# Start addresses of matmul operands: pools at multiples of 128 bytes, and some split weights 64 bytes further

## The chip, the cores and the metric

The kernel runs on one core of one Trainium2 chip. The metric is device time in microseconds (us) of one execution, the median of several runs. A profile is one execution taken with the hardware profiler; all times of single instructions come from it.

TensorE (PE in the profile) multiplies: a matmul holds one operand fixed in the array (the *stationary* operand, 128 columns here, loaded by its own instruction, PEld in the profile) and streams the other through it (the *moving* operand, 256 or 512 columns in nearly all of this kernel). Both are read from SBUF, the on-chip memory of 128 partitions; the sum goes to PSUM. The other engines are VectorE (DVE), ScalarE (ACT), GpSimd (POOL) and SyncE (SP, which only issues DMAs here).

## The reference

A two-layer backbone over 512 latent tokens of width 1024 with 256 context tokens: layer 0 has neighbourhood attention and a bidirectional gated recurrence (HGRN2), layer 1 a gated short convolution, and each layer ends in a convolutional gated feed-forward block. Nearly all the work is in the projections around them:

```python
for layer in range(DEPTH):                       # DEPTH = 2
    h = modulate(rms_norm(x, norm_mix_w[layer]), shift_m, scale_m)
    if is_even:
        y, y_ctx = even_mixer(h, h_ctx, w_in, w_out, rpb, lb, hg_norm_w, ctx_feeds_later)
    else:
        y = short_conv_mixer(h, od_w_in, od_conv_w, od_conv_b, od_w_out)
    x = x + gate_m[:, None, :] * y
    h = modulate(rms_norm(x, norm_ffn_w[layer]), shift_f, scale_f)
    x = x + gate_f[:, None, :] * conv_ffn(h, w_up, conv_w, conv_b, w_down)   # gelu(dwconv3(a)) * val
return rms_norm(x, final_norm_w)
```

All is float32. `conv_ffn` has an up projection to 2 x 2816 columns and a down projection from 2816 rows.

## The kernel before

**Split products.** A float32 operand `a` is split into `hi` (rounded to the matmul's reduced float32 type, `F32R`) and `lo = a - hi`. A product is three matmuls, `hi*hi + hi*lo + lo*hi`. The helper `mm3` (lines 287 to 290) issues them: L288 is weights-hi with moving-hi, L289 weights-hi with moving-lo, L290 weights-lo with moving-hi. So the moving tile alternates between the two halves of one activation, and the weights are loaded anew for each.

**Weights.** `Weights` (lines 41 to 142) walks a list `plan`: each entry is a list of DMA sources and a list of pieces. `_load` (L58) brings an entry into one of two `wraw` tiles by DMA from SP's queue. `conv` (L69) makes the next piece: ACT casts it into a `whi` tile (L92), DVE subtracts into `wlo` (L93); three `whi` and three `wlo` tiles of 128 x 1024 float32 take turns in the pool `wp`. `_block` (L99) does the same for the feed-forward's up projection, which computes a group of columns by Strassen-like combinations (names S1 to S4, A11, A12, A22, W1, W2; L125 and L126 write the split). `HOME` says which blocks share a tile: S1 to A22 lie in two halves of 512 columns of a tile, W1 and W2 each fill one. S1, S2, S3, S4, A11, A12 and A22 meet moving operands of 256 columns (half the tokens), W1 and W2 of 512. Three more pairs of weight tiles, listed in `ws.spare` (L1050), lie in the pool `gq` and are used at the end of each `project_back`.

**Which matmul uses what as weights.** In most stages the split weights are stationary and the activations move: `proj`, `pair`, `project_back` (512 columns; its last piece in two halves of 256), `quad` (two halves of 256) and `group` (the Strassen products). In two places it is turned round, activations stationary and weights moving with 256 columns: the value projection of layer 0 (`pvl`, `pvc`, L577 to L579) and the last down projection (`pd`, L1339 to L1341).

**Order.** Instructions are issued in the order in which the code is written, PE's order included; `Weave` interleaves the attention and recurrence tasks with the projections. Weights are converted a few pieces ahead of the matmuls that use them.

**Addresses.** Tiles of a pool lie one behind the other, each width rounded up to 32 bytes, and pools lie one behind the other too. So a small tile in an early pool moves everything behind it. In the program as built, with offsets in bytes modulo 128: the activations `h`, `hf`, `hm` (pool `yp`), the context `hc` (`mp`), the mixer outputs and most feed-forward outputs `g` (`zp`, `gp`) and the attention operands `KS`, `QS` start at 0; `wraw`, `whi` and `wlo` in `wp` at 64, because the pool `cp` ends at 64; the pools stacked from the other end (`xp`, `fp`, `gq`) at 96, so the Strassen combinations `T2` to `T4`, the spare weight tiles and the first six feed-forward outputs `g` are at 96; the weights `w0h`, `w0l` of the first projection (a temporary pool) at 96 as well.

Of the kernel before, what the change touches and what calls it, by code (L numbers as in the profile page):

```python
# [9 lines left out]
F32 = mybir.dt.float32  # L10
F32R = mybir.dt.float32r
# [3 lines left out]
ALU = mybir.AluOpType  # L15
AX = mybir.AxisListType
PSUM = bass.MemoryType.PSUM

P = 128
D = 1024  # L20
# [3 lines left out]
FF = 2816  # L24
# [17 lines left out]
class Weights:  # L42


    def __init__(self, nc, pool, plan):
        self.nc, self.pool, self.plan = nc, pool, plan
        self.subs = [(c, s) for c, (_, subs) in enumerate(plan) for s in range(len(subs))]
        self.half = {}
        self.raw = {}
        self.ready = []  # L50
        self.nsub = 0
        self.nload = 0
        self.ncall = 0
        self.spare = []
        self.pin = lambda i: i

    def _load(self):
# [8 lines left out]
        self.raw[self.nload] = views  # L66
        self.nload += 1

    def conv(self):  # L69

        if self.nsub >= len(self.subs):
            return
        c, s = self.subs[self.nsub]
        nm = self.plan[c][1][s]
        while self.nload <= min(c + 1 + (nm == "W2"), len(self.plan) - 1):
            self._load()
        if isinstance(nm, str):
            self._block(c, nm)
            return
        i, k0, k1, c0, c1 = self.plan[c][1][s]  # L80
        n, w = k1 - k0, c1 - c0
        if self.spare:
            pool, th, tl = self.spare.pop(0)
            hi = pool.tile([P, 1024], F32R, tag=th, name=f"whi{self.nsub}")
            lo = pool.tile([P, 1024], F32R, tag=tl, name=f"wlo{self.nsub}")
        else:
            hi = self.pool.tile([P, 1024], F32R, tag="whi", name=f"whi{self.nsub}", bufs=3)
            lo = self.pool.tile([P, 1024], F32R, tag="wlo", name=f"wlo{self.nsub}", bufs=3)
        hv = hi[:, : n * w].rearrange("p (k c) -> p k c", c=w)
        lv = lo[:, : n * w].rearrange("p (k c) -> p k c", c=w)  # L90
        rv = self.raw[c][i][:, k0:k1, c0:c1]
        self.nc.scalar.copy(hv, rv)  # L92
        self.pin(self.nc.vector.tensor_tensor(lv, rv, hv.bitcast(F32), ALU.subtract))  # L93
        self.ready.append((hv, lv))
        self.nsub += 1
# [4 lines left out]
    def _block(self, c, nm):  # L100


        V = self.nc.vector
        quarters = self.raw[c][0]
        A21, A22, A11, A12 = (quarters[:, 0, 512 * i : 512 * i + 512] for i in range(4))
        if nm == "S1":
            s3 = self.pool.tile([P, 512], F32, tag="ws3", name=f"ws3{self.nsub}", bufs=1)
            V.tensor_tensor(s3[:], A11, A21, ALU.subtract)
            self.half["S3"] = s3[:]
            V.tensor_tensor(A21, A21, A22, ALU.add)  # L110
        elif nm == "S2":
            V.tensor_tensor(A21, A21, A11, ALU.subtract)
        elif nm == "S4":
            V.tensor_tensor(A21, A12, A21, ALU.subtract)
        if nm in ("W1", "W2"):
            at = 1024 * (nm == "W2")
            src = self.raw[c + 1][0][:, 0, at : at + 1024]
        else:
            src = {"A11": A11, "A12": A12, "A22": A22, "S3": self.half.get("S3")}.get(nm, A21)
        key, z = self.HOME[nm]  # L120
        if z in (None, 0):
            self.half[key] = [self.pool.tile([P, 1024], F32R, tag=t, name=f"{t}{self.nsub}", bufs=3) for t in ("whi", "wlo")]
        at = 512 * (z or 0)
        hi, lo = (t[:, at : at + src.shape[-1]] for t in self.half[key])
        self.nc.scalar.copy(hi, src)  # L125
        V.tensor_tensor(lo, src, hi.bitcast(F32), ALU.subtract)  # L126
        self.ready.append(tuple(t.rearrange("p (g k c) -> p g k c", g=2, c=P) for t in (hi, lo)))
        self.nsub += 1
# [46 lines left out]
def backbone(ctx: ExitStack, tc: tile.TileContext, a, out, dump=None):  # L175
    nc = tc.nc
    V, S, G, TE = nc.vector, nc.scalar, nc.gpsimd, nc.tensor
# [5 lines left out]
    x, ctxt = a["xT"], a["ctxT"]  # L183
    ada_w = a["ada_w"]
    w_in, w_out = a["ev_w_in"][0], a["ev_w_out"][0]
    od_in, od_out = a["od_w_in"][0], a["od_w_out"][0]
    up, down = a["ffn_w_up"], a["ffn_w_down"]


    cp = ctx.enter_context(tc.tile_pool(name="cp", bufs=1))  # L190
    wp = ctx.enter_context(tc.tile_pool(name="wp", bufs=2))
    ap_ = ctx.enter_context(tc.tile_pool(name="ap_", bufs=1))
# [6 lines left out]
    def cols(w, c0):  # L199
        return [([ktiled(w)[:, :, c0 : c0 + 256]], [(0, 0, w.shape[0] // P, j, j + P) for j in (0, P)])]  # L200
# [7 lines left out]
    def wide(w, k0, k1, c0):  # L208
        n = k1 - k0
        return ([ktiled(w)[:, k0:k1, c0 : c0 + 256]], [(0, i, min(i + 4, n), 0, 256) for i in range(0, n, 4)])  # L210

    kgroups = [(0, 6), (6, 14), (14, 22)]
    plan = []
# [8 lines left out]
        plan += cols(w_out, 256 * j)  # L222

    def ffn_up_plan(l):
        r = cols(up[l], 0) + cols(up[l], FF)
        for j in range(FT // 2 - 1):
            q = [a["upq"][l, j, i][:, None, :] for i in range(2)]
            r += [([q[0]], QORDER), ([q[1]], [])]
        return r
# [2 lines left out]
    for j in range(4):  # L232
        plan += [rows_cols(down[0], k0, k1, 256 * j) for k0, k1 in kgroups]
    for j in range(4):
        plan += cols(od_in, D + 256 * j) + cols(od_in, 2 * D + 256 * j) + cols(od_in, 256 * j)
    for j in range(4):
        plan += cols(od_out, 256 * j)
    plan += ffn_up_plan(1)
    for j in range(4):
        plan += [wide(down[1], k0, k1, 256 * j) for k0, k1 in ((0, 8), (8, 16), (16, 22))]  # L240
    ws = Weights(nc, wp, plan)


# [1 line left out]
    ident, sel = cst[:, 0:128], cst[:, 128:256]  # L245
# [11 lines left out]
    oml = cp.tile([P, 8], F32, name="oml")  # L257
    noml = cp.tile([P, 8], F32, name="noml")
    amul = cp.tile([P, 5, KT], F32, name="amul")
    rowv = lambda i, n: pv[:, i : i + n]  # L260


# [211 lines left out]
    class Ada:  # L474
# [3 lines left out]
        n, calls, raw, late = 0, 0, {}, []  # L478
# [9 lines left out]
        def unit(self, aux):  # L488
            self.calls += 1
            while self.late and self.late[0][0] <= self.calls:  # L490
                self.late.pop(0)[1]()
            if self.n >= 8 * len(self.jobs):
                return
            r = self.n % 8
            l, p_, j = self.jobs[self.n // 8]
            while len(self.raw) < min(self.n + 3, 8 * len(self.jobs)):
                self.load()
            raw = self.raw[self.n]
            self.n += 1
            if r == 0:  # L500
                self.acc = ap_.tile([P, T], F32, tag="aacc", name=f"aa{self.n}", bufs=1)
                pin(V.tensor_scalar(self.acc[:], raw[:], sil[:, 0, 0:1], None, ALU.mult))
                return
            pin(V.scalar_tensor_tensor(self.acc[:], raw[:], sil[:, r, 0:1], self.acc[:], ALU.mult, ALU.add))  # L504
            if r < 7:
                return
            red = ap_.tile([P, 16], F32, tag="ared", name=f"ad{self.n}", bufs=1)
            V.tensor_reduce(red[:], self.acc[:].rearrange("p (b j) -> p b j", j=32), axis=AX.X, op=ALU.add,
                            apply_transpose=True)
            pm = []  # L510

            def gather():
                pm.append(aux(f"pad{l}{p_}{j}"))
                TE.matmul(pm[0][:, 0:16], sel, red[:], start=True, stop=True)

            def finish():
                c = p_ * 8 + 4 * j
                for qd in range(4):
                    s4 = slice(32 * qd, 32 * qd + 32)
                    V.tensor_tensor(mod[s4, l, c : c + 4], pm[0][s4, qd:16:4], abT[s4, l * 48 + c : l * 48 + c + 4],  # L520
                                    ALU.add)
                if p_ in (1, 4):
                    w0 = (16 if p_ == 1 else 32) + 8 * l + 4 * j
                    V.scalar_tensor_tensor(amul[:, 2 * l + (1 if p_ == 1 else 2), 4 * j : 4 * j + 4], mod[:, l, c : c + 4],
                                           1.0, pv[:, w0 : w0 + 4], ALU.add, ALU.mult)

            self.late += [(self.calls + 3, gather), (self.calls + 5, finish)]

    ada = Ada()
# [225 lines left out]
    for h in range(4):  # L755
        for d in range(2):
# [3 lines left out]
            s = hp.tile([P, T], F32, tag="s", name=f"s{h}{d}", bufs=2)  # L760
# [209 lines left out]
                wv.tick()  # L970


    xp = ctx.enter_context(tc.tile_pool(name="xp", bufs=1, side="right", reuse_waits="tile"))
    xT = [xp.tile([P, T], F32, name=f"xT{k}") for k in range(KT)]
    for k in range(KT):
        nc.sync.dma_start(xT[k][:], x[k * P : (k + 1) * P, :])
    fp = ctx.enter_context(tc.tile_pool(name="fp", bufs=1, side="right", reuse_waits="tile"))
# [300 lines left out]
    for j in range(4):  # L1278
# [6 lines left out]
        for i in range(2):  # L1285
            t = gp.tile([P, T], F32, tag=f"g{16 + i}", name=f"cs{j}{i}")
# [6 lines left out]
        for i in range(2):  # L1293
            m = 2 * j + i
            V.tensor_tensor(cs[i][:], ou[i][:], cs[i][:], ALU.mult)
            t = fp.tile([P, T], F32, tag="t", name=f"sc{m}", bufs=5)
# [30 lines left out]
    for i in range(4):  # L1327
        for k2 in range(2):
# [1 line left out]
            for k in range(4):  # L1330
                TE.transpose(pt[:, k * P : (k + 1) * P], xT[4 * k2 + k][:, i * P : (i + 1) * P], ident)
            S.copy(xk[i][:, k2 * T : (k2 + 1) * T], pt[:])
    ss = fp.tile([P, 4, 8], F32, tag="ss", name="ssf")

    def down(o, w, i, k0):
        ts = slice(i * P, (i + 1) * P)
# [13 lines left out]
    subs = range(0, FT, 4)  # L1350
# [77 lines left out]
```

## Time and profile before

| | |
|---|---|
| time of three runs | 1332.36 us median (1330.21 to 1336.62) |
| the profiled execution's own time | 1333.99 us |
| its span, first to last instruction | 1332.2 us |
| PE: busy, idle | 1304.5 us, 27.7 us |
| PE weight loads busy | 1147.6 us |
| DVE, ACT, POOL busy | 965.4, 625.2, 84.3 us |
| granted TensorE clock, mean | 0.995 |
| DMA | 172.35 MB, mean 129 GB/s |

The duration that the profile gives for one matmul (0.39 us for 512 columns, 0.28 us for 256) includes its way through the array; matmuls overlap. What the stream costs is the distance from one start to the next, called a *step* below. It is read from the view of stretches, where a row names a stretch of the span, its length, PE's busy time and, behind x, the number of matmuls that touch the stretch. Those that only reach in at an edge are counted too, so the number is one to three above the number of steps.

### The profile page before, as it was taken

Reading aid. Unit: us, or ns where it says so; the run is one execution under the profiler, and the core shown is the slowest. Engines: PE = TensorE matmul, PEld = TensorE weight load, DVE = VectorE, ACT = ScalarE, POOL = GpSimd, SP = SyncE. Lnnn points to the kernel's source line nnn. Section 1 sums busy time; section 2 is a strip of 40 time slices with the busy share of each in tenths; the row PEclk is TensorE's granted clock in tenths of the full one; section 3 lists DMA queues with packets and bytes.
Section 4 is the critical chain, followed back from the end, with each engine's and each line's share of the span. In section 5 each row is a group of like instructions: output and inputs, shape, how many; then the busy total and the mean of one; then the engine's idle time right before and its main releaser. Section 6 shows DMA issues by size and latency. Waiting matters only on the chain. (4 is left out here: it accounts for less than half of the span.)

```text
span 1332.2 us, 21229 instructions
## 1 busy us (share of the span) xinstructions
PE 1304.5 (98%) x8456; PEld 1147.6 (86%) x8456; DVE 965.4 (72%) x1688; ACT 625.2 (47%) x1085; POOL 84.3 (6%) x87
## 2 busy tenths in 40 slices
PE   7999999999999999999999999999999999999997
PEld 4798888888779998889877898888999989899997
DVE  4668897887778878788766776667789897782333
ACT  4443445555545656565422253223456565663223
POOL 2204332311000000000000000000000000000000
PEclk9999999999999999999999999999999999999999
DMA  9842113674562122323466734555403423242231
GB/s 293 265 123 84 33 33 82 152 182 134 153 206 96 64 99 92 127 71 119 141 211 198 226 132 143 167 165 174 158 27 117 142 80 127 80 146 69 91 108 64
DMA packets 134995, 172.35 MB, mean 129 GB/s; under 512 B 14320, under 2 KB 103792, under 8 KB 129776
## 3 DMA queue, kind: packets, MB, share of 16 engines
q1 hardware_dynamic: 132896, 166.15, 39.3%
q10 hardware_dynamic: 2000, 4.85, 1.4%
q8 instruction: 66, 1.08, 0.3%
q14 instruction: 33, 0.27, 0.1%
HBM read 165.21 MB, written 2.10 MB: 126 GB/s over the span
## 5 line engine op out<-in xcount | busy, mean ns | idle before, releaser
L92 ACT CAST whi<-wraw 128x1024 fp32r<-128x1024 f32 (+1 forms) x122 | 124.1, 1021 | 280.8 <-PE pd L1340 70.4
L93 DVE TENSOR_TENSOR wlo<-wraw,whi 128x1024 fp32r<-128x1024 f32 (+1 forms) x122 | 145.2, 1192 | 107.7 <-ACT whi L92 107.1
L288 PE MATMUL p<-hf,whi 128*128 128x512 f32 (+1 forms) x640 | 215.4, 338 | 1.4 <-ACT whi L125 1.4
L290 PE MATMUL p<-hf,wlo 128*128 128x512 f32 (+1 forms) x640 | 214.6, 335 | 0.0
L289 PE MATMUL p<-hf,whi 128*128 128x512 f32 (+1 forms) x640 | 214.1, 335 | 0.0
L125 ACT CAST whi<-wraw 128x512 fp32r<-128x512 f32 (+1 forms) x160 | 113.0, 727 | 85.0 <-PE p L289 35.0
L290 PEld LDWEIGHTS p<-hf,wlo 128*128 128x128 f32 x640 | 120.1, 188 | 13.6
L288 PEld LDWEIGHTS p<-hf,whi 128*128 128x128 f32 x640 | 120.1, 188 | 12.3 <-ACT whi L125 1.6
L289 PEld LDWEIGHTS p<-hf,whi 128*128 128x128 f32 x640 | 120.1, 188 | 10.7
L126 DVE TENSOR_TENSOR wlo<-wraw,whi 128x512 fp32r<-128x512 f32 (+1 forms) x160 | 128.1, 817 | 0.9 <-ACT whi L125 0.5
L504 DVE SCALAR_TENSOR_TENSOR aa<-ar,sil,aa 128x512 f32<-128x512 f32 x140 | 104.8, 749 | 24.1 <-DMA ar<-in_ada_w_dram 21.8
L1339 PE MATMUL pd<-whi,g 128*128 128x256 f32 x352 | 98.2, 279 | 0.0
L1341 PE MATMUL pd<-wlo,g 128*128 128x256 f32 x352 | 98.1, 279 | 0.0
L1340 PE MATMUL pd<-whi,g 128*128 128x256 f32 x352 | 97.9, 278 | 0.0
L288 PE MATMUL pbd<-g,whi 128*128 128x512 f32 (+1 forms) x192 | 73.5, 383 | 0.0
L289 PE MATMUL pbd<-g,whi 128*128 128x512 f32 (+1 forms) x192 | 73.3, 382 | 0.0
L290 PE MATMUL pbd<-g,wlo 128*128 128x512 f32 (+1 forms) x192 | 73.1, 381 | 0.0
L288 PE MATMUL p<-T,whi 128*128 128x256 f32 x240 | 69.0, 288 | 0.0
L290 PE MATMUL p<-T,wlo 128*128 128x256 f32 x240 | 67.2, 280 | 0.0
L289 PE MATMUL p<-T,whi 128*128 128x256 f32 x240 | 67.2, 280 | 0.0
L1340 PEld LDWEIGHTS pd<-whi,g 128*128 128x128 f32 x352 | 66.3, 188 | 0.0
L1339 PEld LDWEIGHTS pd<-whi,g 128*128 128x128 f32 x352 | 66.1, 188 | 0.0
(679 smaller groups left out, 3296.3 us busy)
## 6 DMA issues: line engine op xcount, KB each, us to landing
ar<-in_ada_w_dram SPq DMA_DIRECT2D x160, 256.0 KB, 3.1
wraw<-in_upq_dram SPq DMA_DIRECT2D x40, 1024.0 KB, 4.8
wraw<-in_ffn_w_down_dram SPq DMA_DIRECT2D x16, 1024.0 KB, 5.3
wraw<-in_od_w_in_dram SPq DMA_DIRECT2D x12, 1024.0 KB, 5.6
wraw<-in_ev_w_in_dram SPq DMA_DIRECT2D x20, 512.0 KB, 5.2
araw<-in_ada_w_dram SPq DMA_DIRECT2D x16, 512.0 KB, 6.3
wraw<-in_ffn_w_down_dram SPq DMA_DIRECT2D x8, 768.0 KB, 4.7
wraw<-in_ev_w_out_dram SPq DMA_DIRECT2D x4, 1024.0 KB, 6.9
```

What stands on the lines that cost most here:

```text
L92: self.nc.scalar.copy(hv, rv)
L93: self.pin(self.nc.vector.tensor_tensor(lv, rv, hv.bitcast(F32), ALU.subtract))
L125: self.nc.scalar.copy(hi, src)
L126: V.tensor_tensor(lo, src, hi.bitcast(F32), ALU.subtract)
L288: TE.matmul(o, wh, mh, start=start, stop=False, skip_group_check=True)
L289: TE.matmul(o, wh, ml, start=False, stop=False, skip_group_check=True)
L290: TE.matmul(o, wl, mh, start=False, stop=stop, skip_group_check=True)
L504: pin(V.scalar_tensor_tensor(self.acc[:], raw[:], sil[:, r, 0:1], self.acc[:], ALU.mult, ALU.add))
L1339: TE.matmul(o[i][:, 0:256], gh[:, ts], w[0][:, k - k0], start=k == 0, stop=False)
L1340: TE.matmul(o[i][:, 0:256], gl[:, ts], w[0][:, k - k0], start=False, stop=False)
L1341: TE.matmul(o[i][:, 0:256], gh[:, ts], w[1][:, k - k0], start=False, stop=k == FT - 1)
```

## The change

Nothing is computed differently, and no instruction is added, removed or moved: every engine's sequence holds the same instructions with the same shapes and the same semaphore waits in the same places (7988 matmuls before the compiler splits some of them, for one). What changes is where tiles begin in SBUF.

- An unused tile of 64 bytes (`even`) is put at the end of `cp`, one of 96 bytes (`even2`, in a new pool `ep`) at the other end of SBUF, and two small tiles (`ared`, `ss`) are widened to 128 bytes. With these all the pools named above start at a multiple of 128.
- `whi` and `wlo` tiles in `wp` become 1056 float32 long (4224 bytes, 33 x 128). A piece begins at byte 0 of the tile or, for marked pieces, at byte 64. Marked are plan entries with a third member: the two quads' weights (the first two entries of each feed-forward's up projection, the first two of `od_in`), the last down projection's, and in the Strassen groups all the tiles but those of W1 and W2. The spare tiles in `gq` are not shifted.

```diff
+    SHIFT = 16
+
+    def _part(self, tag, at):
+        return self.pool.tile([P, 1024 + 2 * self.SHIFT], F32R, tag=tag, name=f"{tag}{self.nsub}", bufs=3)[:, at : at + 1024]
...
-            hi = self.pool.tile([P, 1024], F32R, tag="whi", name=f"whi{self.nsub}", bufs=3)
-            lo = self.pool.tile([P, 1024], F32R, tag="wlo", name=f"wlo{self.nsub}", bufs=3)
+            at = self.SHIFT if len(self.plan[c]) > 2 else 0
+            hi, lo = (self._part(t, at) for t in ("whi", "wlo"))
...
-            self.half[key] = [self.pool.tile([P, 1024], F32R, tag=t, name=f"{t}{self.nsub}", bufs=3) for t in ("whi", "wlo")]
+            self.half[key] = [self._part(t, self.SHIFT if z == 0 else 0) for t in ("whi", "wlo")]
...
-        r = cols(up[l], 0) + cols(up[l], FF)
+        r = [e + (1,) for e in cols(up[l], 0) + cols(up[l], FF)]
...
-        plan += cols(od_in, D + 256 * j) + cols(od_in, 2 * D + 256 * j) + cols(od_in, 256 * j)
+        e = cols(od_in, D + 256 * j) + cols(od_in, 2 * D + 256 * j)
+        plan += (e if j else [x + (1,) for x in e]) + cols(od_in, 256 * j)
...
-        plan += [wide(down[1], k0, k1, 256 * j) for k0, k1 in ((0, 8), (8, 16), (16, 22))]
+        plan += [wide(down[1], k0, k1, 256 * j) + (1,) for k0, k1 in ((0, 8), (8, 16), (16, 22))]
...
+    cp.tile([P, 16], F32, name="even")
...
-            red = ap_.tile([P, 16], F32, tag="ared", name=f"ad{self.n}", bufs=1)
+            red = ap_.tile([P, 32], F32, tag="ared", name=f"ad{self.n}", bufs=1)[:, 0:16]
...
+    ep = ctx.enter_context(tc.tile_pool(name="ep", bufs=1, side="right"))
+    ep.tile([P, 24], F32, name="even2")
...
-    ss = fp.tile([P, 4, 8], F32, tag="ss", name="ssf")
+    ss = fp.tile([P, 32], F32, tag="ss", name="ssf")[:, 0:32].rearrange("p (i n) -> p i n", n=8)
```

The matmuls in `F32R` sorted by their columns and by the offsets modulo 128 of both operands, written moving/stationary, in the two built programs:

| matmuls | columns | before | after | where |
|---|---|---|---|---|
| 2592 | 512 | 0/64 | 0/0 | `proj`, `pair`, `project_back`, W1 and W2 |
| 144 | 512 | 96/64 | 0/0 | first `project_back` of a feed-forward (`pbd`), outputs `g` 0 to 5 |
| 144 | 512 | 0/96 | 0/96 | first projection (`pq` with `w0h`, `w0l`) |
| 1248 | 256 | 0/64 | 0/64 | `group` with an `hf` half, half of each `quad` |
| 720 | 256 | 96/64 | 0/64 | `group` with `T2` to `T4` |
| 528 | 256 | 0/64 | 0/0 | context projections, part of the last pieces of `project_back` |
| 432 | 256 | 0/96 | 0/0 | spare weights: half of each `quad`, rest of those last pieces |
| 768 | 256 | 64/0 | 64/0 | `pd`, `g` from 6 up |
| 288 | 256 | 64/96 | 64/0 | `pd`, `g` 0 to 5 |
| 288 | 256 | 64/0 | 0/0 | `pvl`, `pvc` with the weights moving |
| 112 | 256 | 0/0 | 0/0 | attention scores `ps` (L870) |

More of the change, by code (lines that the diff above doesn't have):

```diff
@@ L46, in __init__ @@
         self.nc, self.pool, self.plan = nc, pool, plan
-        self.subs = [(c, s) for c, (_, subs) in enumerate(plan) for s in range(len(subs))]
+        self.subs = [(c, s) for c, e in enumerate(plan) for s in range(len(e[1]))]
         self.half = {}
@@ L506, in unit @@
                 return
-            red = ap_.tile([P, 16], F32, tag="ared", name=f"ad{self.n}", bufs=1)
-            V.tensor_reduce(red[:], self.acc[:].rearrange("p (b j) -> p b j", j=32), axis=AX.X, op=ALU.add,
+            red = ap_.tile([P, 32], F32, tag="ared", name=f"ad{self.n}", bufs=1)[:, 0:16]
+            V.tensor_reduce(red, self.acc[:].rearrange("p (b j) -> p b j", j=32), axis=AX.X, op=ALU.add,
                             apply_transpose=True)
@@ L513, in gather @@
                 pm.append(aux(f"pad{l}{p_}{j}"))
-                TE.matmul(pm[0][:, 0:16], sel, red[:], start=True, stop=True)
+                TE.matmul(pm[0][:, 0:16], sel, red, start=True, stop=True)
             def finish():
```

## Prediction

> **What bounds the kernel now.** I read the page first: busy time by engine and the granted clock.
>
> ```profile
> span 1332.2 us, 21229 instructions
> PE 1304.5 (98%) x8456; PEld 1147.6 (86%) x8456; DVE 965.4 (72%) x1688; ACT 625.2 (47%) x1085; POOL 84.3 (6%) x87
> ...
> PEclk9999999999999999999999999999999999999999
> ```
>
> PE is busy in 1304.5 of 1332.2 us, and its clock is granted from end to end. Next, the waits of PE, longest first.
>
> ```profile
> PE prx L412 <- ACT sqx L410: 5.1, 1, 5.1
> PE pad L514 <- DVE ad L508: 3.7, 2, 1.9
> PE pkc L626 <- DVE sc L609: 2.2, 2, 1.5
> PE pq L288 <- ACT h L312: 1.4, 2, 1.2
> PE p L288 <- ACT whi L125: 1.4, 2, 0.7
> ```
>
> The five longest together are 13.8 us, 5.1 of them before the first matmul. So hardly anything can be won by waking PE earlier; the time is the sum of PE's own steps, and a change of addresses acts only if it changes the step. That is the third reading: stretches with one kind of matmul and nothing between, so that length over number of steps is the step.
>
> ```profile
> 817.78:850.30 32.52, 32.52 (x144) 1.00 0.57 182
> 652.46:660.89 8.43, 8.43 (x38) 1.00 0.28 84
> 61.35:65.10 3.75, 3.75 (x18) 1.00 0.78 285
> 1274.73:1294.45 19.72, 19.72 (x177) 1.00 0.27 92
> 65.33:97.88 32.55, 32.55 (x288) 1.00 0.44 130
> 1294.45:1300.93 6.48, 6.48 (x57) 1.00 0.39 125
> 462.80:466.34 3.54, 3.54 (x31) 1.00 0.00 0
> 406.23:408.84 2.61, 2.61 (x25) 1.00 0.45 188
> 408.84:411.65 2.81, 2.81 (x26) 1.00 0.13 20
> 448.91:450.32 1.41, 1.41 (x13) 1.00 0.00 0
> 366.14:366.98 0.84, 0.84 (x9) 1.00 0.35 44
> ```
>
> With offsets modulo 128 as moving/stationary, from the program's addresses, the rows are in turn:
>
> - 512 columns: 0/64 (`ppb`, `ppc`, `ppu`; 142 steps) 229.0 ns; 96/64 (`pbd`; 36) 234.2 ns; 0/96 (`pq`; 16) 234.4 ns.
> - 256 columns: 64/0 (`pd`; 174) 113.3 ns, and again (`pvl`, `pvc`; 287) 113.4 ns; 64/96 (`pd`; 54) 120.0 ns; 0/64 (`p` with `hf`; 30) 118.0 ns, and another stretch of 0/64 (`pbo`; 23) 113.5 ns; 0/96 (`pbo`, spare weights; 24) 117.1 ns; 96/64 (`p` with `T`; 12) 117.5 ns; 0/0 (`ps`; 7) 120.0 ns.
>
> Rows four and six are the same instruction lines in one loop with the clock at 1.00 in both; only the stationary tile's offset differs, 0 or 96, and the step is 113.3 or 120.0 ns. So the step depends on the two offsets. The shares of DMA (0.27 to 0.44 at 113 ns, 0.00 at 118 ns) do not order the rows.
>
> [...]
>
> **The change part by part.** No instruction moves, so every term is a number of matmuls times a difference of two steps.
>
> *512 columns to 0/0* (2592 from 0/64, 144 from 96/64). No stretch before has this pairing, so the step must be bounded. The weight load cannot set it: the whole 256-column step with its load takes 113.3 ns, less than half of 229.0. What remains is the moving stream and what disturbs it. A disturbance has a measured price: 120.0 - 113.3 = 6.7 ns at 256 columns, 234.2 - 229.0 = 5.2 ns at 512. Two undisturbed 256-column steps are 226.7 ns and contain two starts, where one step of 512 has one; 229.0 is above that, so I read it as disturbed already. One disturbance taken off is 229.0 - 6.7 = 222.3 ns; two are 215.6, the low end. On the high side one more is 235.7. I take 222.3, the single price and the nearest to the 226.7 of the two best 256-column steps. [...] The gain is 2592 x 6.7 = 17.4 us and 144 x 11.9 = 1.7 us.
>
> [...]
>
> *`pd` with `g` 0 to 5*, 64/96 to 64/0: 288 x (120.0 - 113.3) = 1.9 us gained. The other 768 stay.
>
> *`pvl` and `pvc`*, 64/0 to 0/0: these weights are not marked. 288 x (120.0 - 113.4) = 1.9 us lost, by the `ps` row.
>
> *Context projections, last pieces of `project_back`, spare weights*, to 0/0: 528 from 0/64, between 113.5 and 118.0, middle 115.8, so 2.2 us lost (1.1 to 3.4); 432 from 0/96 at 117.1, 1.3 us lost. Were 0/0 harmless there, 2.8 us would be won in place of the 3.5 lost.
>
> *`group` with `T2` to `T4`*, 96/64 to 0/64: 720 from 117.5 to 118.0 or 113.5, so 0.4 us lost to 2.9 us gained. I take 0; the `hf` matmuls of the same groups, which stay at 0/64, mostly keep 118.0.
>
> *Other engines.* ACT, DVE, POOL and the DMAs have new addresses as well. Their instructions hide beside PE, and the stretches show how much room they have.
>
> ```profile
> 107.00:237.00 130.00, 126.15 (x946) 108.89 (x945) 113.36 (x187) 62.80 (x102) 44.58 (x44) 1.00 0.19 50
> 237.00:380.00 143.00, 140.11 (x982) 117.52 (x980) 113.15 (x261) 81.23 (x160) 22.81 (x24) 1.00 0.55 147
> 445.00:665.00 220.00, 220.00 (x1350) 196.89 (x1349) 174.99 (x281) 127.61 (x234) 0.00 (x0) 1.00 0.31 107
> 758.00:968.00 210.00, 210.00 (x1135) 181.31 (x1134) 145.83 (x232) 77.17 (x110) 0.00 (x0) 1.00 0.50 159
> 968.00:1190.00 222.00, 221.26 (x1436) 201.13 (x1435) 186.61 (x319) 130.53 (x243) 0.00 (x0) 1.00 0.28 98
> ```
>
> The columns behind the length are PE, PEld, DVE, ACT, POOL. From 445 to 1190 us DVE, the fullest of the others, is busy 69 to 84%; if PE shortens by 2% it still covers. From 107 to 380 us DVE is at 79 to 87% and PE already waits 6.7 us; 536 of the 512-column matmuls stand there, 3.6 us of the gain. I let 1 us of it be lost to longer waits, and at most 3.6.
>
> **Sum.** 17.4 + 1.7 + 1.9 - 1.9 - 2.2 - 1.3 - 1.0 = 14.6 us. The profiled execution took 1333.99 us, its span 1332.2; from it the changed one is 1319.4. The median of the runs shown lies 1.6 us lower, at 1332.36, so I predict 1317.8, rounded to 1318 us (1.1% faster).
>
> **The rivals.**
>
> 1. *The 512-column step does not care* (it stays at 229.0 for 0/0, and the 144 come down to it from 234.2). Then 0.7 + 1.9 - 1.9 - 3.5 = -2.8, so 1335 us: no change. For it: the 142-step stretch of 0/64 is steady at 229.0 whatever ACT and DVE do, as a cost of the moving stream alone would be. Against it: 96 in place of 64 in the weights alone costs 512 columns 5.4 ns (`pq`), so the loads do reach the stream. [...]
>
> 2. *Slower: 0/0 disturbs 512 columns as it does 256.* [...] Then the step is 235.7: 2592 x 6.7 = 17.4 lost, 144 x 1.5 = 0.2 lost, 3.5 lost as above, 21 us in all, 1353 us. It decides from a step of about 227.9 up, where 2592 x 1.1 and 144 x 6.3 just pay the 3.5. For it: `ps` at 120.0 ns, and the six places where a 512-column matmul at 0 is followed by the load of `QS` at 0; these are the stretches from that matmul to the first `ps`.
>
> ```profile
> 242.05:242.28 0.23, 0.23 (x2) 1.00 0.50 187
> ...
> 350.68:350.92 0.24, 0.24 (x3) 1.00 0.00 0
> sum 1.40, PE 1.40; mean PE 0.23
> ```
>
> Six such steps are 1.40 us, 233 ns each against 229.0, 4 ns more. Against it: each is a single step at a change of shape, out of a stream that ran at 0/64, and a stream in one pairing can settle otherwise: 0/64 itself runs at 113.5 in one stretch and 118.0 in another.
>
> 3. *The change does only part of what it says.* `w0h` and `w0l` keep 96, and the spare tiles, `pvl` and the context stay unshifted; that is in the sum. Should 0/0 be harmless at 256 columns too, the losses of 1.9 and 3.5 us go and 2.8 us are won: 8.2 us more than forecast, 1310 us.
>
> **How the numbers follow.** A run of this kernel can be told from no change at about 0.5%, 6.7 us. I give 0.60 to a 512-column step low enough for a gain beyond that (below about 226), rival 3 included; 0.18 to rival 1 and steps near 229; 0.22 to rival 2, because the six steps and the `ps` row are the only ones with 0/0 and both are high. The likeliest case alone reaches from 1296 (215.6 ns: 34.7 + 2.7 - 3.5 + 2.9 of `T` = 36.8 us) to 1326. The range for all is 1296 to 1340; it leaves out the upper part of rival 2 and a little below, some 0.2. The chances: faster 0.60, same 0.18, slower 0.22.
>
> **What would show it.** In the changed profile, stretches of `ppb`, `ppc` and `ppu` at about 222 ns per step instead of 229.0 bear out the main term; `pd` with low `g` at 113.3 the second, `pvl` at 120.0 the third, `quad` in its two halves at 113 to 118 and 120 the fourth. The forecast is wrong if the 512-column step is at or above 228, if PE is no longer near 98% busy, or if DVE or ACT instructions on the moved tiles change their mean duration.

## The result, and the profile after

The changed kernel takes 1341.37 us (median of 6 runs, 1340.78 to 1344.56), the kernel before in the same comparison 1334.19 us (median of 6, 1330.21 to 1336.62). The ratio is 1.0052, 95% interval 1.0036 to 1.0069: slower by half a per cent, just at the bound above which this kernel's measurement can tell a difference. The forecast was 1318 us with a range from 1296 to 1340, so the sign was wrong and the time lies just above the range.

The head of the profiled execution after (1341.19 us by its own time, 7.2 us over the profiled one before), and PE's longest waits:

```profile
span 1339.4 us, 21229 instructions
PE 1313.4 (98%) x8456; PEld 1149.8 (86%) x8456; DVE 965.9 (72%) x1688; ACT 624.9 (47%) x1085; POOL 84.6 (6%) x87
```

```profile
PE prx L419 <- ACT sqx L417: 5.2, 1, 5.2
PE pad L521 <- DVE ad L515: 3.9, 2, 2.5
PE pkc L633 <- DVE sc L616: 1.8, 2, 1.4
```

Nothing has moved to another engine: DVE, ACT and POOL are busy for as long as before within 0.5 us, and the waits are those of before. PE has 8.9 us more of busy time. So the time is again in PE's steps. Four stretches of the changed kernel in the view of stretches (window; its length; PE busy, with the matmuls that touch it; granted clock; DMA share; GB/s):

```profile
875.59:908.87 33.28, 33.28 (x145) 1.00 0.52 163
1212.42:1332.27 119.85, 119.85 (x1019) 1.00 0.24 78
64.69:98.99 34.30, 34.30 (x289) 1.00 0.41 123
1191.70:1195.75 4.05, 4.05 (x36) 1.00 0.37 104
```

In turn: 143 steps of 512 columns (`ppb`, `ppc` and `ppu`, here and in every row below that is called by one of these names) take 232.7 ns each, where the forecast had 222.3 and before had 229.0. 1017 steps of `pd` take 117.85 ns, whether `g` is low or high; before, high `g` ran at 113.3 and low `g` at 120.0. 288 steps of `pvl` and `pvc` take 119.1 ns (113.4 before). 35 steps of a group with `T` and `hf` take 115.7 ns (117.6 before, the mean over all of this kind). The granted clock is 1.00 in all of them.

Since both programs issue the same 8456 matmuls in one order, each step after can be set against the same step before. Kept here are the pairs in which both steps are back to back (no wait in either):

| matmuls (offsets modulo 128 before, after) | steps | before, ns | after, ns | forecast, us | measured, us |
|---|---|---|---|---|---|
| 512 columns, 0/64 to 0/0 | 2360 | 229.19 | 232.82 | -17.4 | +8.6 |
| 512, 96/64 to 0/0 | 140 | 234.14 | 231.87 | -1.7 | -0.3 |
| 256, `pd` with high `g`, 64/0 kept | 768 | 113.40 | 117.80 | 0 | +3.4 |
| 256, `pd` with low `g`, 64/96 to 64/0 | 272 | 119.96 | 118.00 | -1.9 | -0.5 |
| 256, `pvl`, `pvc`, 64/0 to 0/0 | 287 | 113.43 | 119.13 | +1.9 | +1.6 |
| 256, 0/64 to 0/0 | 495 | 116.39 | 118.64 | +2.2 | +1.1 |
| 256, 0/96 to 0/0 | 424 | 117.57 | 118.77 | +1.3 | +0.5 |
| 256, `T`, 96/64 to 0/64 | 647 | 117.59 | 115.15 | 0 | -1.6 |
| 256, 0/64 kept | 1202 | 116.97 | 116.63 | 0 | -0.4 |

With the few that are not listed this is 12.2 us more. The steps that hold a wait in one of the two traces, or lie in the two stretches of half clock told of next, give 4.9 us back. 3.0 us of these have nothing to do with the change: in the profiled execution before, twice after PE's wait for `pad`, its clock was granted at half for at least 3 us, and in the one after it was not. The two stretches of before:

```profile
669.30:672.30 3.00, 3.00 (x8) 0.50 0.52 163
703.30:706.30 3.00, 3.00 (x8) 0.50 0.74 195
```

The column behind the count is the clock: 0.50, and a 512-column step takes 427 ns there. The repeat of the kernel before, told of below, waits in the same two places and has no such stretch (its clock is 1.00 from 669.30 to 672.30 us and 0.998 in the mean, against 0.995 here), so it comes and goes with the execution. The length of the wait ahead does not decide it alone: the longer of PE's two waits for `pad` was 1.9 us before, and the changed kernel, with one of 2.5 us, kept the full clock. What sets it is not shown.

Two things are to be explained: why the 512-column step rose where the forecast had it fall, and why `pd` with high `g` rose at offsets that the forecast's table calls unchanged.

### The profile page after: what moved, and what is told of

It is laid out like the page before. It is cut to its first block, busy times and chain, and to the rows that moved or that the text cites. A ratio compares the mean times of both kernels' runs of the same rounds, so it can differ in the third digit from the quotient of the medians.

```text
span 1339.4 us, 21229 instructions
## 1 busy us (share of the span) xinstructions
PE 1313.4 (98%) x8456; PEld 1149.8 (86%) x8456; DVE 965.9 (72%) x1688; ACT 624.9 (47%) x1085; POOL 84.6 (6%) x87
## 4 chain that ended last, share of the span: by engine, by line
PE 86%; DVE 7%; DMA 3%; ACT 3%; issue 1%; SPq 0%; ACTq 0%; DVEq 0%
PE p L295 11%; PE p L296 10%; PE p L297 10%; PE pd L1350 3%; PE pd L1348 3%; PE pd L1349 3%; PE pbo L295 2%; PE pbo L297 2%; PE pbo L296 2%; PE pbd L297 2%; PE pbd L296 2%; PE pbd L295 2%; DMA ar<-in_ada_w_dram 2%; PE ppc L297 1%; PE ppc L296 1%; PE ppc L295 1%
## 5 line engine op out<-in xcount | busy, mean ns | idle before, releaser
L1348 PEld LDWEIGHTS pd<-whi,g 128*128 128x128 f32 x352 | 66.5, 189 | 0.0
L1350 PEld LDWEIGHTS pd<-wlo,g 128*128 128x128 f32 x352 | 66.2, 188 | 0.0
```

Of the source, the lines that this page charges most:

```text
L1348: TE.matmul(o[i][:, 0:256], gh[:, ts], w[0][:, k - k0], start=k == 0, stop=False)
L1350: TE.matmul(o[i][:, 0:256], gh[:, ts], w[1][:, k - k0], start=False, stop=k == FT - 1)
```

## The experiments

**Theories.** *Modulo 256:* a step is set by the distance from the start of the moving operand to that of the stationary one, taken modulo 256 bytes and not 128. Then 0/64 before was a distance of 192 throughout, and what the table calls 0/0 after is a distance of 128 or 0, because `whi` and `wlo` tiles of 33 x 128 bytes begin at 0 and at 128 in turn, while the activations came to lie at 128. *Alternation:* the turn makes a step longer than its distances do. *Rival:* 128 bytes are the period, as the prediction read it, and 0/0 is simply worse than 0/64. In the expectations below, A is the rival; B and C are the theory of 256 bytes, C with alternation and D without.

### Where the weights lie, alone: w64, w0, w128

The kernel before, with padding that moves the `wp` pool and nothing else that an `F32R` matmul reads. Its weights are at 192 modulo 256; the three kernels have them at 64, 0 and 128. The diffs:

```diff
+    cp.tile([P, 32], F32, name="even")
+    ap_.tile([P, 32], F32, name="even1")
```

for w64; 16 and 48 in place of 32 and 32 for w0, 48 and 16 for w128.

> The kernel before with 128 bytes of padding ahead of the weight pool and 128 behind the next one: only the split weights and the raw tiles move, from 192 to 64 modulo 256 (64 modulo 128 as before); nothing else changes its place modulo 256. Theory A (only the pairing of the two starts modulo 128 counts): as before, 512-column step 229.0 ns, pd 113.3 ns with high g and 120.0 with low g, time within 0.3% of before. Theory B (the place modulo 256 counts too): the 512-column step differs from 229.0 by 1 ns or more (2.6 us and more in all), and pd from 113.3.

> The same with 64 and 192 bytes: the split weights start at 0 modulo 256, all other operands where they were (0 for the activations). This is the pairing 0/0 for 512 and 256 columns with tiles of equal length. Theory A: the 512-column step is 232.8 ns as in the changed kernel, pd 118 to 120 ns instead of 113.4, 256 columns of proj and group 118 to 120: 9.8 + 6 + 4 us, 1.4% slower than before. Theory B (0/0 is harmless, and in the changed kernel the mixed places of hi and lo tiles modulo 256 cost): 512 columns at or below 229, at most the 256-column steps slower, time within 0.7% of before.

> The same with 192 and 64 bytes: the split weights start at 128 modulo 256, the activations at 0. Theory A: as with the weights at 0 modulo 256, 512-column step 232.8 ns, 1.4% slower than before. Theory B: differs from the kernel with weights at 0 modulo 256 by 1 ns or more per 512-column step.

Measured, against the median of 1336.05 us of the kernel before in that series: w64 1343.99 us, ratio 1.0057 (1.0040 to 1.0075); w0 1344.21 us, 1.0061 (1.0040 to 1.0082); w128 1349.96 us, 1.0104 (1.0082 to 1.0127). In each of the next fences stands `ppb` first (142, 142 and 143 steps), then `pd` with high `g` (174 steps). w64:

```profile
880.40:913.53 33.13, 33.13 (x143) 1.00 0.52 160
1284.22:1303.94 19.72, 19.72 (x176) 1.00 0.28 93
```

w0:

```profile
875.41:907.60 32.19, 32.19 (x144) 1.00 0.53 164
1280.78:1301.65 20.87, 20.87 (x177) 1.00 0.25 86
```

w128:

```profile
881.31:914.54 33.23, 33.23 (x144) 1.00 0.52 163
1290.01:1310.88 20.87, 20.87 (x176) 1.00 0.25 87
```

Steps of 512 columns: 233.3 ns at a distance of 64, 226.7 at 0, 232.4 at 128, against 229.0 at 192 before. w64 has the offsets modulo 128 that the kernel before has, and its step is 4.3 ns longer: the rival of 128 bytes falls. The distance of 0 is the best of all for 512 columns and among the worst for 256: `pd` takes 119.9 ns in w0 and w128, 113.3 in w64 and before. So w0 gains 2.4 us on its 512-column steps (2457 x 0.98 ns, means of the whole trace) and loses 6.8 us in `pd` with high `g`, `pvl` and `pvc` alone.

### The length of the weight tiles, alone: len1088, len1056

len1088 is the changed kernel with tiles of 17 x 256 bytes, so that all of them begin at the same place modulo 256; len1056 is the kernel before with the changed kernel's tile length only, so that they begin at 192 and 64 in turn.

```diff
-        return self.pool.tile([P, 1024 + 2 * self.SHIFT], F32R, tag=tag, name=f"{tag}{self.nsub}", bufs=3)[:, at : at + 1024]
+        return self.pool.tile([P, 1024 + 4 * self.SHIFT], F32R, tag=tag, name=f"{tag}{self.nsub}", bufs=3)[:, at : at + 1024]
```

```diff
-            hi = self.pool.tile([P, 1024], F32R, tag="whi", name=f"whi{self.nsub}", bufs=3)
-            lo = self.pool.tile([P, 1024], F32R, tag="wlo", name=f"wlo{self.nsub}", bufs=3)
+            hi = self.pool.tile([P, 1056], F32R, tag="whi", name=f"whi{self.nsub}", bufs=3)
+            lo = self.pool.tile([P, 1056], F32R, tag="wlo", name=f"wlo{self.nsub}", bufs=3)
...
-            self.half[key] = [self.pool.tile([P, 1024], F32R, tag=t,
+            self.half[key] = [self.pool.tile([P, 1056], F32R, tag=t,
```

> The changed kernel with weight tiles of 1088 instead of 1056 float32 (4352 bytes, 17 x 256, instead of 33 x 128): all whi and wlo tiles then have the same place modulo 256 (0, or 64 where marked), where the changed kernel has half of them 128 further. Theory A: no difference to the changed kernel, 512-column step 232.8, pd 117.9, 0.5% slower than before. Theory B: pd back from 117.9 to 113.4 ns (4.7 us) and the 512-column step down from 232.8 towards 229 (up to 9.8 us): faster than the changed kernel by 0.4 to 1.1%.

> The kernel before with weight tiles of 1056 instead of 1024 float32 and nothing else: neighbouring whi and wlo tiles then alternate between 192 and 64 modulo 256, no start is moved modulo 128. Theory C (the difference of the two starts modulo 256 sets a step, and hi and lo tiles in different places cost on top): 512-column step 231.5 to 233 instead of 229.2, pd with high g about 117 instead of 113.4; 6 to 13 us, 0.5 to 1.0% slower. Theory D (each step has the price of its own difference, alternation is free): 1560 of the 512-column matmuls keep 229.2 and 1032 get 233.2, mean 230.8, pd stays at 113.4 to 114.7; 4 to 5 us, 0.3% slower. Theory A (modulo 128): no change.

Measured: len1088 1340.74 us, ratio 1.0037 (1.0024 to 1.0051); len1056 1343.98 us, 1.0070 (1.0051 to 1.0089). len1088, with `ppb` (142 steps), `pd` (174) and `pbd` with low `g` (36):

```profile
876.74:909.75 33.01, 33.01 (x144) 1.00 0.52 161
1310.01:1329.73 19.72, 19.72 (x177) 1.00 0.07 27
655.17:663.38 8.21, 8.21 (x38) 1.00 0.27 85
```

`ppb` is at a distance of 128 and takes 232.5 ns, as in w128, where the weights and not the activations had moved: it is the distance that counts. `pbd` has a distance of 0 (its `g` 0 to 5 begin at 0 as the weights do) and takes 228.1 ns. `pd` is back at 113.3. So `pd` in the changed kernel has its 4.4 ns from the length of the tiles. Its 512-column step was expected to fall towards 229 and did not: len1088 has all of them at 128, one of the two bad distances. len1056, with `ppc` (142 steps of 512 columns) and `pd` (174):

```profile
877.69:910.75 33.06, 33.06 (x143) 1.00 0.50 160
1281.83:1302.32 20.49, 20.49 (x176) 1.00 0.27 88
```

These 512-column steps are at 192 and 64 in turn and take 232.8 ns. Over the whole trace those at 192 take 231.2 ns (229.2 before) and those at 64 take 232.0 (233.2 in w64): each lies between the two values that they have alone. (Where distances take turns, a step is put down to the matmul that begins at its end.) `pd` takes 117.8. The tile length alone makes the kernel slower by 0.7%, about as much as the whole change. In the changed kernel the turn costs more at 512 columns: the steps at a distance of 0 take 232.0 ns (975 steps) where w0 has 228.2, and those at 128 take 233.4 (1391 steps) where w128 has 232.5, so both are above their values alone. Sorted by both matmuls of a step, the changed kernel's trace shows where this comes from: from 0 to 0 a step takes 228.4 ns (182 steps) and from 128 to 128 it takes 232.7 (699), as alone; from 0 to 128 it takes 233.9 (763) and from 128 to 0 it takes 232.7 (862). So the loss is in the steps that change the distance. Of the 512-column matmuls that came from 0/64, 1032 lie at 0 and 1560 at 128 after; by the distances alone (228.2 and 232.5 ns) they would average 230.8 ns, 1.6 above the 229.2 of before, and the other 2.0 of the measured 232.8 come with the turn. len1056 does not follow this simple rule: from 192 to 192 it takes 232.9 ns (673 steps), where before has 229.2.

### Without the shift of 64 bytes: unmarked

```diff
-            at = self.SHIFT if len(self.plan[c]) > 2 else 0
+            at = 0
...
-            self.half[key] = [self._part(t, self.SHIFT if z == 0 else 0) for t in ("whi", "wlo")]
+            self.half[key] = [self._part(t, 0) for t in ("whi", "wlo")]
```

> The changed kernel with no piece moved by 64 bytes (tiles stay 1056 float32 long): pools at multiples of 128 alone. Theory C: the 1968 marked matmuls of group and quad go from 116 to 118.5 to 119.5 ns and the 1056 of pd from 117.9 to about 119.5; 5 to 9 us more than the changed kernel, 0.9 to 1.2% slower than before; the 512-column step stays at 232.8. Theory A says the same of these, so this run only prices the marking.

Measured: 1348.89 us, ratio 1.0102 (1.0084 to 1.0121). The same 1017 steps of `pd`, and `ppb` (143 steps):

```profile
1216.79:1337.82 121.03, 121.03 (x1019) 1.00 0.24 77
878.07:911.35 33.28, 33.28 (x145) 1.00 0.51 162
```

`pd` takes 119.0 ns instead of 117.85, and over the trace the 256-column steps that had 0/64 before take 118.9 instead of 117.2. So the shift does help: it is worth about half a per cent (1.0102 against 1.0052, each against the kernel before in its own series), and of the three parts that were tried alone (length, shift, right side) it is the only one with a gain. `ppb` has the same 232.7 ns with it and without.

### Everything at 0 modulo 256, and the right side alone: p256m, right0

p256m is len1088 with 128 bytes more of padding, which brings the activations to 0 modulo 256, and with the value projection's weights marked too. Its 512-column matmuls are at a distance of 0, its marked 256-column ones at 64 or 192.

```diff
-        return self.pool.tile([P, 1024 + 2 * self.SHIFT], F32R, tag=tag, name=f"{tag}{self.nsub}", bufs=3)[:, at : at + 1024]
+        return self.pool.tile([P, 1024 + 4 * self.SHIFT], F32R, tag=tag, name=f"{tag}{self.nsub}", bufs=3)[:, at : at + 1024]
...
-        plan.append(wide(w_in, 0, 8, 3072 + 256 * j))
+        plan.append(wide(w_in, 0, 8, 3072 + 256 * j) + (1,))
...
+    ap_.tile([P, 32], F32, name="even1")
```

right0 is the kernel before with `even2` and `ss` of the change only: `T2` to `T4`, the spare weights and `g` 0 to 5 come to 0, the weights stay at 192.

> The changed kernel with tiles of 1088 float32, 128 bytes of padding in the pool ap_ and the value projection's weights marked too: every operand starts at 0 modulo 256, marked weights at 64. Theory C: the 2736 matmuls of 512 columns at difference 0 take 228.2 ns (before 229.2 and 234.1: -3.5 us), group and quad at difference 64 about 116.2 (-1.8 us), pd 114 to 115 (-1 us), the 960 unmarked ones of 256 columns 119.5 (+2.3 us): 0.3% faster than before, 0.8% faster than the changed kernel. Theory A: the same starts modulo 128 as the changed kernel, so 512-column step 232.8 and pd 117.9, 0.5% slower than before.

> The kernel before with only the pools of the other end moved (even2 and the wider ss): T2 to T4, the first six g and the spare weight tiles start at 0 instead of 96, all else stays. Both theories: pd with low g 113.4 instead of 120.0 (288: -1.9 us), the pbd steps of 512 columns 229.2 instead of 234.1 (144: -0.7 us), T about 117 as before, spare weights 119.5 instead of 117.6 (432: +0.8 us): -1.8 us, 0.1% faster, which five rounds may just not tell from no change.

Measured: p256m 1336.00 us, ratio 1.0012 (1.0001 to 1.0022); right0 1335.24 us, 0.9997 (0.9986 to 1.0007). p256m, with `ppb` (142 steps) and `pd` (1017):

```profile
872.28:904.46 32.18, 32.18 (x143) 1.00 0.52 164
1208.82:1328.60 119.78, 119.78 (x1020) 1.00 0.24 78
```

right0, with `pvl` and `pvc` (287 steps) and `pd` (1017):

```profile
65.23:97.79 32.56, 32.56 (x289) 1.00 0.45 130
1206.64:1326.42 119.78, 119.78 (x1019) 1.00 0.24 78
```

The 512-column step is the best again, 226.6 ns. In p256m the distance is 0 and 256 in turn when it is counted modulo 512, and the steps from 0 to 0 (177) and from 256 to 256 (699) take 227.7 and 228.3 ns, so no longer period shows. Yet p256m isn't the 0.3% faster that was expected of it. `pd` takes 117.8 ns in both kernels, where the theory of 256 bytes had 114 to 115 and 113.4, for 1017 steps on end, and in right0 it has the very offsets (192 moving, 0 stationary) at which it took 113.3 before. The same offsets give 113.4 ns in `pvl` and `pvc` of the same trace. So at a distance of 64 or 192 a 256-column step has two values, 113.3 and 117.8, and keeps one for long. What was different before is what ran ahead of it: the steps of low `g`, at a distance of 160 and 120.0 ns, before each of the long stretches at 113.3. In right0 there are none. That is a theory to be tried:

### What runs ahead: right0k, p192, p192k, again

right0k is right0 with the first `g` tile alone put at 96 bytes, so that 48 steps of `pd` are at a distance of 160, three at a time. Four such threes, nine steps apart, stand ahead of each of the four long stretches of `pd`:

```diff
+        if f == 0:
+            t = gq.tile([P, 2 * T + 64], F32R, tag="q0", name=f"g{l}0")
+            return t[:, 24 : 24 + T], t[:, 24 + T : 24 + 2 * T]
```

p192 is p256m with a shift of 192 bytes instead of 64 (tiles still 1088 long), and p192k is p192 with the weights of the first of the twelve stages of `pd` (96 matmuls) at 96 bytes, again a distance of 160:

```diff
-            at = self.SHIFT if len(self.plan[c]) > 2 else 0
+            at = (self.plan[c] + (0,))[2] and (self.SHIFT if self.plan[c][2] == 1 else 24)
...
-        plan += [wide(down[1], k0, k1, 256 * j) + (1,) for k0, k1 in ((0, 8), (8, 16), (16, 22))]
+        plan += [wide(down[1], k0, k1, 256 * j) + (1 if j or k0 else 2,) for k0, k1 in ((0, 8), (8, 16), (16, 22))]
```

again is the kernel before, unchanged.

> The kernel with the right side alone at multiples of 128 (right0, ratio 0.9997), and in it the first gated tile of each feed-forward network 96 bytes further, so that the first steps of pd load a stationary operand 160 bytes (modulo 256) from the moving one: 48 matmuls in all. In right0 all of pd lay at a difference of 64 and its last 1017 steps in a row took 117.8 ns; in the kernel before the same pairing took 113.3 ns, and steps at the difference 160 stood ahead of it. If a stretch keeps the one of two steps that it was put in by what ran ahead: pd at 113.3 ns after the first tile, 1296 x 3.5 ns = 4.5 us less than right0, 0.3 us of it lost on the 48, ratio about 0.997. If what ran ahead does not matter: pd stays at 117.8 ns and the ratio at 1.000.

> All operand places at 0 modulo 256 and tiles of 1088 values (p256m, ratio 1.0012), but weights of 256-column matmuls 192 bytes further instead of 64. If only the distance from a multiple of 128 counts, nothing changes: 512 columns at 228.0, pd at 117.8, group and quad matmuls at 117.7 ns, ratio 1.001. If the differences 64 and 192 modulo 256 have the same two steps, and the place in the run decides, pd and the group matmuls take 113.3 or 117.8 ns: with pd alone at 113.3, 1344 x 4.45 = 6.0 us less (0.997), with both, 1968 x 4.3 = 8.5 us more gone (0.990).

> p192, and the weights of the first of the twelve stages of pd in the second network at 96 bytes instead of 192, a difference of 160 to the gated tiles, for 96 matmuls. If steps at the difference 160 put what follows on the faster of the two steps: pd at 113.3 ns from there, 960 x 4.45 = 4.3 us under p192 if p192 has pd at 117.8 there, the 96 at about 120 ns (0.2 us more), ratio about 0.998 if the group matmuls stay at 117.7. If what ran ahead does not matter, as p192.

> The kernel before, unchanged, profiled in another execution. If the faster of the two steps of the 256-column matmuls is set by the program's own history, the same stretches have it again: pd at 113.3 ns from about 1214 us on, pd low g at 120.0, the group matmuls in the same proportion of 113.3 and 117.7 (mean 116.8). If it is chance, the stretches differ: pd anywhere between 113.3 and 117.8.

Measured, against 1334.23 us: right0k 1331.16 us, ratio 0.9969 (0.9957 to 0.9980); p192 1336.14 us, 1.0008 (0.9997 to 1.0020); p192k 1331.33 us, 0.9970 (0.9958 to 0.9982); again 1333.18 us, one run. One of the four long `pd` stretches of right0k (225 steps), then two of p192: 15 steps near the beginning of `pd`, and its last 1017:

```profile
1267.26:1292.76 25.50, 25.50 (x227) 1.00 0.26 84
```

```profile
1195.09:1196.79 1.70, 1.70 (x18) 1.00 0.69 279
1204.91:1324.69 119.78, 119.78 (x1019) 1.00 0.24 78
```

and of p192k, the 58 last steps at a distance of 160, then the 959 that follow them:

```profile
1203.88:1210.83 6.95, 6.95 (x60) 1.00 0.34 103
1210.83:1319.54 108.71, 108.71 (x962) 1.00 0.24 79
```

right0k is at 113.3, p192 at 117.8, p192k at 119.8 and then 113.4 to the end of `pd`. In p192k fewer than a hundred steps at another distance decide on 4.4 ns of each of the thousand behind them, and both kernels with such steps came out near the ratio expected of that theory (0.997 and 0.998 expected, 0.997 measured for both). p192 itself took as long as p256m and has the same 117.8, the first of the two outcomes written down for it. But its trace also shows that steps at 160 are not needed: the 15 steps of its first row take 113.3 ns at the same offsets as its last 1017. Between the two, small matmuls (`pgb`, `pxk`) break the stream, and it comes back at 117.8. So one pairing has both values in one execution, and what decides between them can lie in the matmuls that run just ahead of a stream. right0k and p192k both beat the kernel before and the changed one. The repeat of the kernel before, with high `g` (174 steps) and the 54 steps of low `g` behind them:

```profile
1213.16:1232.88 19.72, 19.72 (x177) 1.00 0.27 91
1232.88:1239.36 6.48, 6.48 (x57) 1.00 0.38 121
```

113.3 and 120.0 again, and the means of every kind of step with over a hundred of them agree with the first execution within 0.5 ns, most of them within 0.15: in this one repeat it is the program that sets the value, not chance.

## Why the prediction was wrong, point by point

- **PE's steps set the time, and addresses set the steps:** right; w64 and w0 have the same instructions at 233.3 and at 226.7 ns. The clock was not granted "from end to end": the row of digits hides the two stretches of 3 us at half, but they bear on no step in the sum.
- **"With offsets modulo 128":** this is the step that failed. For 512 columns the period is 256: a step is 233.3 ns at a distance of 64 (w64) and 229.0 at 192. All 512-column matmuls at 0/64 before were at a distance of 192; the change put them at 128 and 0, neither of which the trace before had for them, and the table of offsets showed the prediction neither that nor the turn of the tiles between the two.
- **"I take 222.3":** wrong in sign, 232.8 after, and +8.6 us where -17.4 was forecast. That 0/0 takes the price of one disturbance off a 512-column step was the author's estimate, and no run shows 222.3 ns. The 26.0 us of this term are more than the whole gap of 21.8 us between the forecast sum (-14.6) and the two profiled executions (+7.2). Even the best distance would not have borne it out: the lowest 512-column stretch of any run is 226.6 to 226.7 ns, which is just twice 113.3, the value that the prediction named and passed by. So 2.3 ns could be taken off 229.0, and not 6.7. At 228.1 for all (p256m's mean) 2592 steps gain 2.9 us.
- **"The other 768 stay":** wrong, +3.4 us. Their offsets modulo 128 did stay, but by the new tile length their distances are 64 and 192 in turn (len1056 does the same, len1088 undoes it). The mean of 117.8 is that of the upper value in right0, but the single steps are not alike: 113 to 124 ns in the changed kernel, 117 to 119 in right0. So the two need not have one cause.
- **`pd` with low `g` to 113.3:** half right; it came down from 120.0, to 118.0.
- **`pvl`, `pvc` and the other 256-column steps to 0/0:** right in sign and smaller in size, 3.2 us lost where 5.4 were forecast (120.0 was taken, 118.6 to 119.1 measured). The half of `quad` that kept 0/64 rose too, from 114.4 to 118.9 ns, over the 118 that was forecast as its most.
- **`T`, taken as 0:** 1.6 us gained, inside the bounds given.
- **Waits longer by 1.0 us:** they became shorter. Of the 4.9 us, 3.0 are the half clock of the profiled execution before. PE's idle time fell from 27.7 to 26.0 us, which is most of the rest; that a slower PE leaves shorter waits is likely, but was not shown.
- **The rivals:** the second one came true in its direction, and its deciding point (a step above 227.9) held. Its 235.7 ns and 1353 us were too high. Its evidence, six steps of 233 ns ahead of `ps`, were six steps at 0/0 modulo 256, so a single step between two kinds of matmul priced neither the stretches at a distance of 0 (226.7) nor those at 128 (232.4). That it was given 0.22 and the forecast 0.60 follows from the reading modulo 128.

Three things stay open. Why a step that changes from a distance of 0 to 128 or back is slower wasn't settled. Of what decides between 113.3 and 117.8 only one thing was tried, steps at 160 ahead of `pd`; it isn't the only one, since `pd` is at 113.3 in len1088 and w64 too, which have none. What the kernels at 113.3 have in common is that some steps of `pd` lie at another distance than the long stretch (192 in len1088, 32 in w64, 160 in the others), while right0, p256m and p192, with one distance for all of `pd`, end at 117.8; that this is the rule was not tested. And what in the two operand reads makes the distance matter at all is not shown by any run.

## What to carry to other kernels

Before addresses are changed, list the start of both operands for every kind of matmul modulo at least 256 (the 512-column step of this kernel took 226.7 ns at 0 and 232.4 at 128), from the built program, and treat a pairing that the trace doesn't contain as unknown, to be measured by a padding of a few bytes before a kernel is rebuilt around it. Tiles that take turns should have a length that is a multiple of that period; otherwise the pairing changes from piece to piece (len1056, 0.7% slower). And a step read from one stretch may be one of two values that the same pairing can have (113.3 and 117.8 ns for `pd`), so compare it with other stretches and other programs before it goes into a sum.

## What the runs showed of the hardware

Steps of these `F32R` matmuls with a new weight load each, by the distance from the moving to the stationary operand modulo 256 (means of the back-to-back steps of the trace named, clock 1.00; in the last row the 256-column steps at 32, 160 and 224 are those of `pd` alone):

| distance | 512 columns, ns | 256 columns, ns |
|---|---|---|
| 0 | 228.2 (w0; 226.7 in long stretches) | 119.5 (w0) |
| 64 | 233.2 (w64) | 113.3 or 117.8 |
| 128 | 232.5 (w128, len1088) | 118.7 (w128; `pd` 120.0) |
| 192 | 229.2 (before) | 113.3 or 117.8 |
| 32, 96, 160, 224 | 233.2, 234.1, 233.7, 233.2 (w128, before, w0, w64) | 118.3, 117.6, 120.0, 116.7 (w64, before, before, w128) |

The best distance for 512 columns (0, 226.7 ns) is among the worst for 256 (119.5 ns). With one start at 0 for all weights in `wp`, w0 takes 1.0061 of the time before; with a second start for marked weights p256m takes 1.0012, p192 1.0008 and p192k 0.997. The period of 256 is read from the 512-column steps: at 256 columns 64 and 192 have the same two values, and 0 and 128 differ by about 1 ns. Not every value holds in every program: a distance of 96 gave 117.6 ns before and 119.5 in w64 (424 steps, outside `pd`). Two starts in turn (128 and 0) brought the step at 0 from 228.2 to 232.0 ns. And a 256-column stream at 64 or 192 runs at 113.3 or 117.8 ns for a thousand steps, and steps at another distance ahead of it changed which (p192k against p192).
